# Residual add and RMSNorm on one core: every transfer in 64 KiB runs, a residual area of 9 rows, gamma in PSUM

## The chip, the cores and the metric

The kernel runs on one core of a Trainium2 chip. The metric is the device time of one launch in microseconds (us), the median of several runs. All runs named here are fast, at a granted clock of 1.0, so that they can be compared directly.

## The reference

```python
# x, residual: (32, 2048, 2048) float32; gamma: (2048,) float32; eps = 1e-6
z = x + residual
rms = np.sqrt(np.mean(z ** 2, axis=-1, keepdims=True) + eps)
return (z / rms * gamma).astype(np.float32)
```

There are 65,536 rows of 2048 elements. Two tensors of 537 MB are read and one is written, 1610.6 MB in all.

## The kernel before

A tile is 8 rows on each of 128 partitions, 64 KiB per partition; there are 64 tiles. SBUF holds two z slots (x arrives in one, is worked on in place, and is stored from it) and one residual slot, 192 KiB of each partition; there is no third z slot and no second residual slot. All large transfers go out from one queue, SP's, in program order.

```python
z_slots = [slots.tile([P, R, D], fp32, name=f"z{k}") for k in range(2)]   # R = 8, D = 2048
r_slot = slots.tile([P, R, D], fp32, name="r_slot")
gamma_tile = slots.tile([P, D], fp32, name="gamma_tile")
# ... cut
def load_r(i):
    nc.sync.dma_start(out=r_slot, in_=r_t[i])              # 64 KiB run per partition
def load_x(i):                                             # two halves of 32 KiB
    z = z_slots[i % 2]
    for h in range(2):
        s = slice(h * H, (h + 1) * H)                      # H = 4
        nc.sync.dma_start(out=z[:, s, :], in_=x_t[i][:, s, :])
def compute(i):
    z = z_slots[i % 2]
    for h in range(2):
        s = slice(h * H, (h + 1) * H)
        nc.vector.tensor_add(out=z[:, s, :], in0=z[:, s, :], in1=r_slot[:, s, :])
        # ... cut: 4 squares with a sum on ScalarE, then a square root
    for h in range(2):
        # ... cut: reciprocal, then 4 in-place multiplications by rstd and gamma on VectorE
# ... cut: the first two tiles
for i in range(1, n_tiles):
    store(i - 1)
    compute(i)
    if i + 1 < n_tiles:
        load_r(i + 1)      # waits until the adds of tile i have read r_slot
        load_x(i + 1)      # waits until store(i - 1) has left the z slot
store(n_tiles - 1)
```

In the steady state the DMA engines work through a round of three things per tile: x of tile i, the store of tile i-1, the residual of tile i+1. When x of tile i has landed, the store of tile i-1 is the only work left in the queue until the residual load is issued, and that waits for the adds.

Of the kernel before, what the change touches and what calls it, by code (L numbers as in the profile page):

```python
# [1 line left out]

# [4 lines left out]


@with_exitstack
def kernel(  # L10
    ctx: ExitStack,
    tc: tile.TileContext,
    x: bass.AP,
    residual: bass.AP,
    gamma: bass.AP,
    eps: float,
    out: bass.AP,
):




    nc = tc.nc
    P = nc.NUM_PARTITIONS
    fp32 = mybir.dt.float32
    Act = mybir.ActivationFunctionType
    mult = mybir.AluOpType.mult

    x_f = x.flatten_outer_dims()
    r_f = residual.flatten_outer_dims()  # L30
    o_f = out.flatten_outer_dims()

    n_rows, D = x_f.shape
    R = 8
    H = R // 2
    assert n_rows % (P * R) == 0
    n_tiles = n_rows // (P * R)
    assert n_tiles >= 3

    x_t = x_f.rearrange("(n p r) m -> n p r m", p=P, r=R)  # L40
    r_t = r_f.rearrange("(n p r) m -> n p r m", p=P, r=R)
    o_t = o_f.rearrange("(n p r) m -> n p r m", p=P, r=R)

    inv_d = 1.0 / float(D)

    slots = ctx.enter_context(tc.tile_pool(name="slots", bufs=1))
    stats = ctx.enter_context(tc.tile_pool(name="stats", bufs=3))
    psum = ctx.enter_context(tc.tile_pool(name="psum", bufs=1, space=bass.MemoryType.PSUM))

    z_slots = [slots.tile([P, R, D], fp32, name=f"z{k}") for k in range(2)]  # L50
    r_slot = slots.tile([P, R, D], fp32, name="r_slot")
    gamma_tile = slots.tile([P, D], fp32, name="gamma_tile")
    eps_tile = slots.tile([P, 1], fp32, name="eps_tile")
    sq_junk = psum.tile([P, D], fp32, name="sq_junk")
    nc.vector.memset(eps_tile, float(eps))  # L55

    def load_r(i):
        nc.sync.dma_start(out=r_slot, in_=r_t[i])  # L58

    def load_x(i):  # L60
        z = z_slots[i % 2]
        for h in range(2):
            s = slice(h * H, (h + 1) * H)
            nc.sync.dma_start(out=z[:, s, :], in_=x_t[i][:, s, :])  # L64

    def store(i):
        z = z_slots[i % 2]
        if i < n_tiles - 1:
            nc.sync.dma_start(out=o_t[i], in_=z)
            return  # L70
        for h in range(2):
            s = slice(h * H, (h + 1) * H)
            nc.sync.dma_start(out=o_t[i][:, s, :], in_=z[:, s, :])

    def compute(i):
        z = z_slots[i % 2]
        rstds = []
        for h in range(2):
            s = slice(h * H, (h + 1) * H)
            nc.vector.tensor_add(out=z[:, s, :], in0=z[:, s, :], in1=r_slot[:, s, :])  # L80
            ssq = stats.tile([P, H], fp32, name=f"ssq{h}")
            for g in range(H):
                nc.scalar.activation(  # L83
                    out=sq_junk,
                    in_=z[:, h * H + g, :],
                    func=Act.Square,
                    accum_out=ssq[:, g : g + 1],
                )
            rms = stats.tile([P, H], fp32, name=f"rms{h}")
            nc.scalar.activation(out=rms, in_=ssq, func=Act.Sqrt, bias=eps_tile, scale=inv_d)  # L90
            rstds.append((rms, stats.tile([P, H], fp32, name=f"rstd{h}")))
        for h in range(2):
            rms, rstd = rstds[h]
            nc.vector.reciprocal(out=rstd, in_=rms)  # L94
            for g in range(H):
                row = z[:, h * H + g, :]
                nc.vector.scalar_tensor_tensor(  # L97
                    out=row,
                    in0=row,
                    scalar=rstd[:, g : g + 1],  # L100
                    in1=gamma_tile,
                    op0=mult,
                    op1=mult,
                )


    def load_gamma():
        nc.vector.memset(gamma_tile, 0.0)  # L108
        for q in range(4):
            nc.scalar.dma_start(  # L110
                out=gamma_tile[32 * q : 32 * q + 1, :], in_=gamma.partition_broadcast(1)
            )
        nc.vector.stream_shuffle(gamma_tile, gamma_tile, [0] * 32)  # L113

    load_r(0)
    load_x(0)
    load_gamma()
    load_x(1)
    compute(0)
    load_r(1)  # L120
    for i in range(1, n_tiles):
        store(i - 1)
        compute(i)
        if i + 1 < n_tiles:
            load_r(i + 1)
            load_x(i + 1)
    store(n_tiles - 1)


# [1 line left out]
_INS = ['x', 'residual', 'gamma', 'eps']  # L131
_OUTS = [((32, 2048, 2048), 'float32')]

_NUMBERS = {'eps': 9.999999974752427e-07}


# [26 lines left out]
```

## Time and profile before

| what | value |
|---|---|
| time, median of 3 runs | 3733.61 us (3733.6 to 3735.15) |
| VectorE / ScalarE busy | 62% / 29% |
| SP's DMA queue | 99.9% of the 16 engines' span |
| one steady round (25.17 MB) | 58.06 us |

Three lines of the page: the DMA's busy tenths in 40 slices of the span, the GB/s in the same slices, and the SP queue (packets, MB, share of the 16 engines' span).

```profile
DMA  9999999999999999999999999999999999999999
GB/s 425 414 437 430 435 433 431 435 435 432 433 431 435 436 430 437 429 436 433 431 436 430 437 432 431 437 430 439 430 432 434 432 437 431 430 435 436 431 435 389
...
q1 hardware_dynamic: 37008, 1610.63, 99.9%
```

The DMA is busy in every slice and moves about 433 GB/s in the middle. The kernel is bound by moving bytes.

The timeline of one steady round. The columns are start, duration, engine (SPq is SP issuing a transfer), source line, operation, tiles, and in brackets the idle time before and what ended it.

```profile
1831.38 8.69 DVE L80 TENSOR_TENSOR z<-z,r_slot 128x8192 f32<-128x8192 f32 x1 [1.01 <-DMA z<-in_x_dram]
...
1840.11 0.33 SPq L58 DMA_DIRECT2D r_slot<-in_residual_dram  x1
...
1850.70 0.80 SPq L64 DMA_DIRECT2D z<-in_x_dram  x2
...
1858.63 0.34 SPq L69 DMA_DIRECT2D out_dram<-z  x1
1879.84 8.69 DVE L80 TENSOR_TENSOR z<-z,r_slot 128x8192 f32<-128x8192 f32 x1 [21.24 <-DMA z<-in_x_dram]
...
1889.45 8.69 DVE L80 TENSOR_TENSOR z<-z,r_slot 128x8192 f32<-128x8192 f32 x1 [0.91 <-DMA z<-in_x_dram]
```

The second half of x has landed at 1831.38 and its add takes 8.69 us. The residual load (L58) is issued right behind it, 8.7 us after the add's start. The x loads (L64) follow when the old store is done, the next store (L69) at 1858.63, and at 1889.45 the round begins again, 58.07 us later.

### The profile page before, as it was taken

The numbers are of one execution on the slowest core, as the hardware profiler recorded it, in microseconds if no ns is written. First come the engines' busy times: TensorE is split into PE (matmuls) and PEld (weight loads), VectorE is DVE, ScalarE is ACT, GpSimd is POOL, SyncE is SP. The second block draws the span as 40 slices with busy tenths as digits, with TensorE's granted clock in tenths as the row PEclk, the third lists the DMA queues.
The fourth block names the chain that finished last, engine by engine and source line by source line (L and its number), as shares of the span: only waits on it lengthen the run. The fifth ranks groups of instructions, "written<-read, shape, count | busy, mean of one in ns | idle before, by whom it ended". The sixth has DMA issues, their size and how long they took to land.

```text
span 3732.7 us, 2427 instructions
## 1 busy us (share of the span) xinstructions
DVE 2298.0 (62%) x772; ACT 1066.4 (29%) x1154; POOL 0.2 (0%) x4
## 2 busy tenths in 40 slices
DVE  5665655656557565575655756657566575665756
ACT  2331322313223132231322313323233232331322
POOL 0000000000000000000000000000000000000000
DMA  9999999999999999999999999999999999999999
GB/s 425 414 437 430 435 433 431 435 435 432 433 431 435 436 430 437 429 436 433 431 436 430 437 432 431 437 430 439 430 432 434 432 437 431 430 435 436 431 435 389
DMA packets 37035, 1610.82 MB, mean 432 GB/s; under 512 B 4116, under 2 KB 4116, under 8 KB 4116
## 3 DMA queue, kind: packets, MB, share of 16 engines
q1 hardware_dynamic: 37008, 1610.63, 99.9%
q14 instruction: 19, 0.16, 0.0%
q10 hardware_dynamic: 8, 0.03, 0.0%
HBM read 1073.77 MB, written 536.87 MB: 431 GB/s over the span
## 4 chain that ended last, share of the span: by engine, by line
DMA 66%; another core or an unknown queue 16%; DVE 16%; SPq 1%; ACT 0%; issue 0%; DVEq 0%
DMA z<-in_x_dram 64%; DVE z L80 15%; DMA out_dram<-z 1%; DVE z L97 1%; DMA r_slot<-in_residual_dram 1%; SPq L64 1%; SPq L58 0%; ACT sq_junk L83 0%; DVE rstd L94 0%; DVEq L158 0%; ACT L90 0%; ACT rms L90 0%; DVEq L80 0%
## 5 line engine op out<-in xcount | busy, mean ns | idle before, releaser
L80 DVE TENSOR_TENSOR z<-z,r_slot 128x8192 f32<-128x8192 f32 x128 | 1112.5, 8692 | 1395.0 <-DMA z<-in_x_dram 1382.5
L83 ACT ACTIVATE sq_junk<-z 128x2048 f32<-128x2048 f32 x512 | 963.5, 1882 | 2635.0 <-DVE z L80 2622.9
L97 DVE SCALAR_TENSOR_TENSOR z<-z,rstd,gamma_tile 128x2048 f32<-128x2048 f32 x512 | 1169.9, 2348 | 4.5
L83 ACT ACTIVATION_READ_ACCUMULATOR sq_junk<-z 128x1 f32 x512 | 95.8, 187 | 0.0
L90 ACT ACTIVATE rms<-ssq,eps_tile 128x4 f32<-128x4 f32 x128 | 38.1, 298 | 4.1
L94 DVE RECIPROCAL rstd<-rms 128x4 f32<-128x4 f32 x128 | 21.9, 171 | 0.1
L113 DVE LOAD_MASK_SELECT gamma_tile<-gamma_tile x1 | 0.0, 14 | 21.2 <-DMA gamma_tile<-in_gamma_dram 21.2
L83 ACT ACT_TABLE_LOAD x1 | 1.3, 1283 | 4.4 <-issue 4.4
L113 DVE STREAM_SHUFFLE gamma_tile<-gamma_tile 128x2048 f32<-128x2048 f32 x1 | 2.4, 2419 | 0.0
L108 DVE MEMSET gamma_tile<- 128x2048 f32 x1 | 1.8, 1765 | 0.4 <-issue 0.4
L90 ACT ACT_TABLE_LOAD x1 | 1.3, 1283 | 0.0
L55 DVE MEMSET eps_tile<- 128x1 f32 x1 | 0.1, 59 | 0.8 <-PEq L144 0.8
L144 POOL MEMSET const-bfloat16-1.0<- 128x1 bf16 x1 | 0.1, 103 | 0.0
L144 POOL MEMSET const-uint8-127<- 128x1 uint8 x1 | 0.1, 103 | 0.0
L144 POOL MEMSET const-float32-1.0<- 128x1 f32 x1 | 0.1, 100 | 0.0
L144 POOL MEMSET const-float32-0.0<- 128x1 f32 x1 | 0.1, 99 | 0.2 <-issue 0.2
## 6 DMA issues: line engine op xcount, KB each, us to landing
z<-in_x_dram SPq DMA_DIRECT2D x128, 4096.0 KB, 38.3
out_dram<-z SPq DMA_DIRECT2D x2, 4096.0 KB
r_slot<-in_residual_dram SPq DMA_DIRECT2D x64, 29.9
out_dram<-z SPq DMA_DIRECT2D x63, 50.1
gamma_tile<-in_gamma_dram ACTq DMA_DIRECT2D x4, 8.0 KB
```

The lines of the kernel that those rows point to most:

```text
L55: nc.vector.memset(eps_tile, float(eps))
L64: nc.sync.dma_start(out=z[:, s, :], in_=x_t[i][:, s, :])
L80: nc.vector.tensor_add(out=z[:, s, :], in0=z[:, s, :], in1=r_slot[:, s, :])
L83: nc.scalar.activation(out=sq_junk, in_=z[:, h * H + g, :], func=Act.Square, accum_out=ssq[:, g : g + 1],)
L90: nc.scalar.activation(out=rms, in_=ssq, func=Act.Sqrt, bias=eps_tile, scale=inv_d)
L94: nc.vector.reciprocal(out=rstd, in_=rms)
L97: nc.vector.scalar_tensor_tensor(out=row, in0=row, scalar=rstd[:, g : g + 1], in1=gamma_tile, op0=mult, op1=mult,)
L108: nc.vector.memset(gamma_tile, 0.0)
L113: nc.vector.stream_shuffle(gamma_tile, gamma_tile, [0] * 32)
L144: nc = _bacc.Bacc("TRN2", target_bir_lowering=False, num_devices=1)
```

## The change

The intent is to make every large transfer one 64 KiB run per partition, so x now comes in one piece. The add can then no longer begin at the first half, and the residual load would come very late. So the residual area gets a ninth row: tiles use its rows 0 to 7 and 1 to 8 in turn, and the one row that the next load does not overwrite is added last. The load has to wait for 7 rows instead of 8. The extra row takes the SBUF of gamma, which moves to PSUM. The first and the last tile are cut into pieces of 2 rows.

```diff
-    r_slot = slots.tile([P, R, D], fp32, name="r_slot")
-    gamma_tile = slots.tile([P, D], fp32, name="gamma_tile")
+    r_area = slots.tile([P, R + 1, D], fp32, name="r_area")
+    gamma_tile = psum.tile([P, D], fp32, name="gamma_tile")
     def load_r(i):
-        nc.sync.dma_start(out=r_slot, in_=r_t[i])
+        a = i % 2
+        nc.sync.dma_start(out=r_area[:, a : a + R, :], in_=r_t[i])
-    def load_x(i):
+    def load_x(i, piece=R):
         z = z_slots[i % 2]
-        for h in range(2):
-            s = slice(h * H, (h + 1) * H)
+        for a in range(0, R, piece):
+            s = slice(a, a + piece)
             nc.sync.dma_start(out=z[:, s, :], in_=x_t[i][:, s, :])
     def compute(i):
+        if i % 2 == 0:
+            order = list(range(1, R)) + [0]
+            add(i, 1, R)
+            add(i, 0, 1)
+        else:
+            order = list(range(R))
+            add(i, 0, R - 1)
+            add(i, R - 1, R)
+        groups = (order[:4], order[4:])
+        rms = [square(i, g) for g in groups]
+        for g, m in zip(groups, rms):
+            scale(i, g, m)
# ... cut: add, square and scale as functions, the old body of compute,
#     gamma staged in the area's last row, the first and last tile by pieces of 2 rows
```

More of the change, by code (lines that the diff above doesn't have):

```diff
@@ L34 @@
     R = 8
-    H = R // 2
     assert n_rows % (P * R) == 0
@@ L46 @@
     slots = ctx.enter_context(tc.tile_pool(name="slots", bufs=1))
-    stats = ctx.enter_context(tc.tile_pool(name="stats", bufs=3))
+    stats = ctx.enter_context(tc.tile_pool(name="stats", bufs=4))
     psum = ctx.enter_context(tc.tile_pool(name="psum", bufs=1, space=bass.MemoryType.PSUM))
     z_slots = [slots.tile([P, R, D], fp32, name=f"z{k}") for k in range(2)]
-    r_slot = slots.tile([P, R, D], fp32, name="r_slot")
-    gamma_tile = slots.tile([P, D], fp32, name="gamma_tile")
+    r_area = slots.tile([P, R + 1, D], fp32, name="r_area")
@@ L64, in load_x, with store @@
             nc.sync.dma_start(out=z[:, s, :], in_=x_t[i][:, s, :])
-    def store(i):
+    def store(i, piece=R):
         z = z_slots[i % 2]
-        if i < n_tiles - 1:
-            nc.sync.dma_start(out=o_t[i], in_=z)
-            return
-        for h in range(2):
-            s = slice(h * H, (h + 1) * H)
-            nc.sync.dma_start(out=o_t[i][:, s, :], in_=z[:, s, :])
-    def compute(i):
-        z = z_slots[i % 2]
-        rstds = []
-        for h in range(2):
-            s = slice(h * H, (h + 1) * H)
-            nc.vector.tensor_add(out=z[:, s, :], in0=z[:, s, :], in1=r_slot[:, s, :])
-            ssq = stats.tile([P, H], fp32, name=f"ssq{h}")
-            for g in range(H):
-                nc.scalar.activation(
-                    out=sq_junk,
-                    in_=z[:, h * H + g, :],
-                    func=Act.Square,
-                    accum_out=ssq[:, g : g + 1],
-                )
-            rms = stats.tile([P, H], fp32, name=f"rms{h}")
-            nc.scalar.activation(out=rms, in_=ssq, func=Act.Sqrt, bias=eps_tile, scale=inv_d)
-            rstds.append((rms, stats.tile([P, H], fp32, name=f"rstd{h}")))
-        for h in range(2):
-            rms, rstd = rstds[h]
-            nc.vector.reciprocal(out=rstd, in_=rms)
-            for g in range(H):
-                row = z[:, h * H + g, :]
-                nc.vector.scalar_tensor_tensor(
-                    out=row,
-                    in0=row,
-                    scalar=rstd[:, g : g + 1],
-                    in1=gamma_tile,
-                    op0=mult,
-                    op1=mult,
-                )
@@ new lines, in store, with add, square @@
+        for a in range(0, R, piece):
+            s = slice(a, a + piece)
+            nc.sync.dma_start(out=o_t[i][:, s, :], in_=z[:, s, :])
+    def add(i, a, b):
+        z = z_slots[i % 2]
+        o = i % 2
+        nc.vector.tensor_add(
+            out=z[:, a:b, :], in0=z[:, a:b, :], in1=r_area[:, a + o : b + o, :]
+        )
+    def square(i, rows):
+        z = z_slots[i % 2]
+        ssq = stats.tile([P, 4], fp32, name="ssq")
+        for k, g in enumerate(rows):
+            nc.scalar.activation(
+                out=sq_junk, in_=z[:, g, :], func=Act.Square, accum_out=ssq[:, k : k + 1]
+            )
+        n = len(rows)
+        rms = stats.tile([P, 4], fp32, name="rms")
+        nc.scalar.activation(
+            out=rms[:, :n], in_=ssq[:, :n], func=Act.Sqrt, bias=eps_tile, scale=inv_d
+        )
+        return rms
@@ new lines, in scale @@
+    def scale(i, rows, rms):
+        z = z_slots[i % 2]
+        n = len(rows)
+        rstd = stats.tile([P, 4], fp32, name="rstd")
+        nc.vector.reciprocal(out=rstd[:, :n], in_=rms[:, :n])
+        for k, g in enumerate(rows):
+            nc.vector.scalar_tensor_tensor(
+                out=z[:, g, :],
+                in0=z[:, g, :],
+                scalar=rstd[:, k : k + 1],
+                in1=gamma_tile,
+                op0=mult,
+                op1=mult,
+            )
+    def compute(i):
+        if i % 2 == 0:
[10 more added lines that the diff above has]
+            scale(i, g, m)
@@ L107, in load_gamma, with compute_by_pieces @@
+    def compute_by_pieces(i):
+        groups = [list(range(a, a + 2)) for a in range(0, R, 2)]
+        before = None
+        for g in groups:
+            add(i, g[0], g[-1] + 1)
+            m = square(i, g)
+            if before is not None:
+                scale(i, *before)
+            before = (g, m)
+        scale(i, *before)
     def load_gamma():
-        nc.vector.memset(gamma_tile, 0.0)
+        stage = r_area[:, R, :]
+        nc.vector.memset(stage, 0.0)
         for q in range(4):
@@ L110, in load_gamma @@
             nc.scalar.dma_start(
-                out=gamma_tile[32 * q : 32 * q + 1, :], in_=gamma.partition_broadcast(1)
+                out=r_area[32 * q : 32 * q + 1, R, :], in_=gamma.partition_broadcast(1)
             )
-        nc.vector.stream_shuffle(gamma_tile, gamma_tile, [0] * 32)
+        nc.vector.stream_shuffle(gamma_tile, stage, [0] * 32)
     load_r(0)
-    load_x(0)
+    load_x(0, 2)
     load_gamma()
     load_x(1)
-    compute(0)
+    compute_by_pieces(0)
     load_r(1)
+    last = n_tiles - 1
@@ L121 @@
     for i in range(1, n_tiles):
         store(i - 1)
-        compute(i)
-        if i + 1 < n_tiles:
+        if i < last:
+            compute(i)
             load_r(i + 1)
-            load_x(i + 1)
-    store(n_tiles - 1)
+            load_x(i + 1, 2 if i + 1 == last else R)
+    compute_by_pieces(last)
+    store(last, 2)
 _INS = ['x', 'residual', 'gamma', 'eps']
```

## The prediction

> **What bounds the kernel now.** The DMA engines. The page's slices show DMA at 9 in all 40; its queue table gives the SP queue 99.9% of the 16 engines' span. The chain that ended last is 66% DMA. VectorE is busy 62%, ScalarE 29%. From tile 3 on, the timeline repeats every 58.06 us (59.0 in a few tiles): 25.17 MB per tile, 433 GB/s. The Trainium skill (page "DMA: Bandwidth & Descriptors", section "Where 436 GB/s comes from") puts the ceiling at 435 GB/s; the trace agrees. The same bytes must still move, so little can be won: 1610.6 MB at 435 GB/s is 3701 us (estimate).
>
> **What the change removes.**
> 1. Run length. The packet records show 64 KiB packets at 2418 ns and 32 KiB packets at 1215 ns (medians). A group of 8 x packets and its semaphore write takes 9.70 us on an engine, twice that 19.41; a group of 8 packets of 64 KiB takes 19.32. Only x changes. Saved: about 0.09 us per tile, 62 tiles, 5.5 us, all on the critical path.
> 2. The gap near 100 us. The engines idle 0.7 to 1.7 us there, since the load of r(2) is issued only at 100.42 us, when both adds of tile 1 are done. With 7 rows (about 15.2 us at the measured 8.69 us for 4) in place of 8 (17.3 us) it comes 2 us earlier: about 1 us saved.
> 3. The end. Most engines run dry 7 to 8 us before the last stores, but the two slowest only 1.0 and 2.4 us. With stores of 2 rows the first ones are ready early and the queue never dries: 1 us, set by the slowest engine.
>
> **What it adds.** Shorter runs in the first and last tile: 0.3 us. The scaling reads gamma from PSUM (2.35 us each now): I expect 2.3 to 2.4.
>
> **What it moves.** x arrives as one transfer, so the add can't start at the first half: the residual load is issued about 15.8 us after x has landed, against 8.7 now, and its first packet follows about 1 to 1.5 us later. Meanwhile the store of the tile before keeps the queue fed for 19.3 us. The slack shrinks from about 9 to some 2 us. The slowest engine should not idle; engines that run ahead by more than 2 us will, harmlessly, but pulled together they may stall each other more, as they do in the first 500 us (extra 0.2 to 1 us on first packets of x). Allowance: 0 to 4 us. The tile's store is issued about 42 us after x lands (27 now), still before the DMA needs it at 58.
>
> **Predicted:** 3733.6 - 5.5 - 1 - 1 + 0.3 + about 1 = 3727 us; 8 in 10 between 3721 and 3733. Faster by over 2%: 1%; within 2%: 97%; slower by over 2%: 2%.
>
> **What would show it.** Step 1: packets down from 37,035 to about 29,000 and a period near 57.97 us between the large adds. Step 2: no idle near 100 us. Step 3: all engines busy through the last 20 us, DMA 9 in the last slice, last store landing about 40 us after the last x piece. Slack: residual loads issued 15 to 16 us after the large add starts; DMA share still 1.00 in the middle.
>
> **What would make it wrong.** The residual load waiting for both adds, or for ScalarE (1 us dry in each tile is 1.7%); stalls from engines held in step; or 64 KiB loads of x being slower than those of the residual.

## The result, and the profile after

| | before | after |
|---|---|---|
| median | 3733.8 us | 3796.97 us |
| range, 6 runs each | 3733.6 to 3735.15 | 3793.44 to 3801.55 |
| ratio | | 1.0169 (95% interval 1.0156 to 1.0182) |

Ratios here and below are the mean time of one kernel's fast runs over that of the other's of the same rounds, so they are not quite the ratio of the medians. The change made the kernel 1.7% slower: 63 us more, and 70 us above the prediction and well outside its range. The interval is clear of 1.

The same three lines of the page after the change:

```profile
DMA  9999999999999999999999999999999999999999
GB/s 419 427 425 430 430 430 428 418 429 424 421 422 423 428 420 426 426 418 428 429 427 426 417 423 426 422 425 424 425 423 424 429 428 425 424 418 424 420 424 403
...
q1 hardware_dynamic: 28944, 1610.63, 99.7%
```

Fewer packets move the same bytes, as intended, and the DMA is still busy in every slice. Only the rate has fallen, to about 424 GB/s. The busy share hides the loss, because a packet that is held up counts as busy. The windows view of the long middle stretch says it more plainly (stretch, length, the busy time and count of VectorE, ScalarE and GpSimd, granted clock, DMA share, GB/s), before and then after:

```profile
1000.00:3000.00 2000.00, 1232.92 (x410) 571.77 (x619) 0.00 (x0) 1.00 1.00 434
```

```profile
1000.00:3000.00 2000.00, 1206.64 (x403) 545.59 (x597) 0.00 (x0) 1.00 1.00 424
```

The DMA share is 1.00 in both, at 434 and 424 GB/s. One steady round after the change:

```profile
1799.65 17.29 DVE L78 TENSOR_TENSOR z<-z,r_area 128x14336 f32<-128x14336 f32 x2 [16.68 <-DMA z<-in_x_dram]
1814.76 0.33 SPq L61 DMA_DIRECT2D r_area<-in_residual_dram  x1
...
1818.96 0.33 SPq L67 DMA_DIRECT2D z<-in_x_dram  x1
...
1841.85 0.34 SPq L73 DMA_DIRECT2D out_dram<-z  x1
1858.55 17.29 DVE L78 TENSOR_TENSOR z<-z,r_area 128x14336 f32<-128x14336 f32 x2 [16.73 <-DMA z<-in_x_dram]
```

The residual load (L61) is now issued 15.1 us after the add's start instead of 8.7, the store 42.2 us instead of 27.2. The large add starts 58.90 us after the last one in this round; the mean over the steady rounds is 59.30 (in the profiled execution, which at 3801.55 us was the slowest of the six).

The packet records (start, duration and size of every packet) and the semaphore writes at the end of each engine's share (a semaphore is the counter that tells the waiting engine that data have landed) say where in the round it goes. From these I took the mean time that the 16 engines need for each transfer. After the change x takes 20.07 us, the store 19.33, the residual 19.91. A clean transfer of this size takes 19.32 to 19.35. So x loses 0.7 us and the residual 0.6 us per round, on all engines and mostly as longer packets: at the start of the residual load, and in the last two or three packets of the x load that comes after it.

The records also show that the 16 engines are not in step. "Spread" below is the time between the first and the last engine's end of the same transfer. "Lead" is the time from the issue of the residual load until the first engine has finished the store in front of it.

| | before | after |
|---|---|---|
| spread, early and late in the run | 1.6 and 7.8 us | 1.4 to 3.3 us, without a trend |
| lead of the residual load over the first engine | 4.6 us (mean) | 1.3 us |
| the same over the slowest engine | 10.1 us | 3.8 us |

The slowest engine always has its next work in time, as the prediction said. The round slows down nevertheless. Hardly any engine even runs dry: the first packet follows 0.96 us after the issue, and in the mean only 0.6 of the 16 engines per round have a lead below that.

### The profile page after: what moved, and what is told of

Read it like the earlier page. It is cut to its first block, busy times and chain, and to the rows that moved or that the text cites. A ratio compares the mean times of both kernels' runs of the same rounds, so it can differ in the third digit from the quotient of the medians.

```text
span 3799.8 us, 2509 instructions
## 1 busy us (share of the span) xinstructions
DVE 2296.1 (60%) x780; ACT 1060.1 (28%) x1158; POOL 0.2 (0%) x4
## 4 chain that ended last, share of the span: by engine, by line
DMA 64%; DVE 29%; ACT 7%; issue 0%; DVEq 0%; SPq 0%
DMA z<-in_x_dram 33%; DMA out_dram<-z 30%; DVE z L102 15%; DVE z L78 13%; ACT sq_junk L86 7%; DMA r_area<-in_residual_dram 1%; ACT rms L91 0%; DVE rstd L100 0%; DVEq L191 0%; ACT L91 0%; DVEq L78 0%; SPq L61 0%; SPq L67 0%
## 5 line engine op out<-in xcount | busy, mean ns | idle before, releaser
L78 DVE TENSOR_TENSOR z<-z,r_area 128x14336 f32<-128x14336 f32 (+2 forms) x132 | 1107.5, 8429 | 1066.6 <-DMA z<-in_x_dram 1049.2
L102 DVE SCALAR_TENSOR_TENSOR z<-z,rstd,gamma_tile 128x2048 f32<-128x2048 f32 x512 | 1167.9, 2343 | 4.5
L100 DVE RECIPROCAL rstd<-rms 128x4 f32<-128x4 f32 (+1 forms) x132 | 22.7, 173 | 391.3 <-ACT rms L91 391.3
L91 ACT ACTIVATE rms<-ssq,eps_tile 128x4 f32<-128x4 f32 (+1 forms) x132 | 39.2, 297 | 4.3
```

Source lines behind the costliest of these rows:

```text
L78: nc.vector.tensor_add(out=z[:, a:b, :], in0=z[:, a:b, :], in1=r_area[:, a + o : b + o, :])
L91: nc.scalar.activation(out=rms[:, :n], in_=ssq[:, :n], func=Act.Sqrt, bias=eps_tile, scale=inv_d)
L100: nc.vector.reciprocal(out=rstd[:, :n], in_=rms[:, :n])
L102: nc.vector.scalar_tensor_tensor(out=z[:, g, :], in0=z[:, g, :], scalar=rstd[:, k : k + 1], in1=gamma_tile, op0=mult, op1=mult,)
```

## The experiments

Theory A: the residual load comes too late. Its rival, theory B: the 64 KiB runs of x are what stalls where the queue turns from loads to stores. Eleven kernels were run, named e1 to e12 (there is no e6). The first four tell the two theories apart. The diffs are shortened: repeated branches and lines of the first tiles are left out.

**e1: x in halves again, the late residual load kept.**

```diff
-            load_x(i + 1, 2 if i + 1 == last else R)
+            load_x(i + 1, 2 if i + 1 == last else R // 2)
```

> The changed kernel with x loaded again as two transfers of 4 rows (32 KiB per partition), and nothing else put back: the add of 7 rows still waits for both, so the residual load is still issued about 15.5 us after x has landed. Theory A (the late residual load: engines that run ahead go dry, are pulled back into step, and all 16 then stall together where the queue turns from loads to stores and back): stays slow, 3780 to 3805 us, spread between the engines 1.5 to 3 us. Theory B (the 64 KiB runs of x are themselves what stalls at the turn): back to 3730 to 3745 us.

Measured: 3803.91 us, ratio 1.0185 (1.0170 to 1.0200). The runs of x were put back and nothing was won. Theory B falls. The load still goes out 15.1 us after the add's start, as this round of e1 shows:

```profile
1866.52 17.29 DVE L78 TENSOR_TENSOR z<-z,r_area 128x14336 f32<-128x14336 f32 x2 [17.73 <-DMA z<-in_x_dram]
1881.64 0.33 SPq L61 DMA_DIRECT2D r_area<-in_residual_dram  x1
```

**e2: x whole, the residual early.**

```diff
     def load_r(i):
-        a = i % 2
-        nc.sync.dma_start(out=r_area[:, a : a + R, :], in_=r_t[i])
+        for h in (0, R // 2):
+            s = slice(h, h + R // 2)
+            nc.sync.dma_start(out=r_area[:, s, :], in_=r_t[i][:, s, :])
     def compute(i):
-        add(i, 1, R); add(i, 0, 1)                  # or 0..7 and 7..8
+        add(i, 0, R // 2); add(i, R // 2, R)
# ... cut: in add, the residual is read from a fixed place
```

> The changed kernel with x still as one transfer of 64 KiB per partition, but the residual at a fixed place, added in two adds of 4 rows and loaded in two transfers of 4 rows, each issued when its add is done: the first about 9 us after x has landed, as early as in the kernel before. Theory A: back to 3722 to 3738 us, the spread between engines grows to 5 us and more. Theory B: stays at 3770 to 3800 us.

Measured: 3729.66 us (3729.32 to 3730.19), ratio 0.9987 (0.9970 to 1.0004). The large runs of x stay and the loss is gone. From the timeline of e2:

```profile
1826.56 17.29 DVE L79 TENSOR_TENSOR z<-z,r_area 128x8192 f32<-128x8192 f32 x2 [22.35 <-DMA z<-in_x_dram]
1835.28 8.93 SPq L62 DMA_DIRECT2D r_area<-in_residual_dram  x2
...
1884.57 17.30 DVE L79 TENSOR_TENSOR z<-z,r_area 128x8192 f32<-128x8192 f32 x2 [22.22 <-DMA z<-in_x_dram]
```

The first half of the residual is issued 8.7 us after the add's start, as early as before the change, and the round is back at 58.0 us. The spread grew to more than 6 us.

**e3: the kernel before, with one add of 8 rows.**

```diff
-            nc.vector.tensor_add(out=z[:, s, :], in0=z[:, s, :], in1=r_slot[:, s, :])
+            if h == 0:
+                nc.vector.tensor_add(out=z, in0=z, in1=r_slot)
```

> The kernel before with only this changed: one add of 8 rows when both halves of x are there, so the residual load is issued about 17.5 us after x has landed instead of 8.7. All runs as in the kernel before (x 32 KiB, the rest 64 KiB). Theory A: as slow as the changed kernel or slower, 3795 to 3900 us. Theory B: 3730 to 3745 us.

Measured: 4011.26 us, ratio 1.0731 (1.0707 to 1.0754). Nothing of the change is in this kernel except the lateness, and it loses 277 us, more than expected. The middle stretch of e3 in the windows view:

```profile
1000.00:3000.00 2000.00, 1146.89 (x353) 528.11 (x576) 0.00 (x0) 1.00 0.96 403
```

Here the engines really are idle at times (share 0.96). The load is issued 1.6 us after the first engine has run dry, yet 1.7 us before the slowest engine is done. Its transfer takes 22.6 us in the mean of all engines. In this, 15 of the 16 wait for their first packet, 2.2 us in the mean; but the slowest one, which has its work in time, takes 22.4 us too instead of 19.3.

**e4: x in halves, each added as it lands, all else as changed.**

```diff
# on top of e1
-            add(i, 1, R)
+            add(i, 1, R // 2)
+            add(i, R // 2, R)
             add(i, 0, 1)
# and in the other branch
-            add(i, 0, R - 1)
+            add(i, 0, R // 2)
+            add(i, R // 2, R - 1)
```

> The changed kernel with x in two halves and the adds split so that each half is added as it lands; gamma in PSUM, the area of 9 rows, and the first and last tile by pieces of 2 rows all stay. The residual load is issued 6.5 to 8.7 us after x has landed. Both theories: 3725 to 3737 us. If it stays above 3745 us, one of the parts left in (gamma in PSUM, the pieces, the area) costs time, and both theories fall.

Measured: 3731.35 us (3731.17 to 3731.5), ratio 0.9991 (0.9976 to 1.0006). The ninth row, gamma in PSUM and the pieces at both ends cost nothing. e1 and e4 differ in when the add begins, and so when the residual goes out: 73 us lie between them. Two rounds of e4, with the load 6.6 and 8.7 us after the start of the last large add:

```profile
1828.29 8.76 DVE L78 TENSOR_TENSOR z<-z,r_area 128x6144 f32<-128x6144 f32 x2 [0.90 <-DMA z<-in_x_dram]
1834.88 0.33 SPq L61 DMA_DIRECT2D r_area<-in_residual_dram  x1
...
1886.45 8.69 DVE L78 TENSOR_TENSOR z<-z,r_area 128x8192 f32<-128x8192 f32 x1 [0.85 <-DMA z<-in_x_dram]
1895.17 0.33 SPq L61 DMA_DIRECT2D r_area<-in_residual_dram  x1
```

The next four ask how the lateness works.

**e5: x as 2 and 6 rows, an intermediate lateness.** The residual lies at a fixed place and the adds follow the pieces.

```diff
-        for a in range(0, R, piece):
-            s = slice(a, a + piece)
+        cuts = [0, 2, R] if piece == R else list(range(0, R + 1, piece))
+        for a, b in zip(cuts, cuts[1:]):
+            s = slice(a, b)
             nc.sync.dma_start(out=z[:, s, :], in_=x_t[i][:, s, :])
# compute: add(i, 0, 2); add(i, 2, R)
```

> The changed kernel with x as two transfers of 2 and 6 rows, added in the same parts as they land, and the residual at a fixed place: the residual load goes out 13.0 us after x has landed, between the 8.7 of the kernel before and the 15.2 of the changed one. Theory A, in the form that it has now: a residual load costs time once it comes later than the moment when the first engine has done the store before it. That is at 19.3 us less its latency (0.96 us in the traces) less the 0.5 us from landing to the add less the spread of the engines: for 13.0 us, only at a spread over 4.9 us. So 3728 to 3740 us, and the spread grows to about 5 us and stays there. If instead the loss grew evenly with the lateness, it would be near 3765 us.

Measured: 3740.34 us, ratio 1.0017 (1.0002 to 1.0032): just over what theory A had, and far from an even growth with lateness. The spread stayed at 3.3 to 4.4 us instead of 5, so the allowance that I had made for the load's latency was too small. The mean lead over the first engine is 2.3 us. Most rounds are clean (median 58.08 us) and some are not (mean 58.30).

**e7: GpSimd adds two of the seven rows.** All runs stay at 64 KiB.

```diff
-            add(i, 1, R)
+            add(i, R - 2, R, nc.gpsimd)
+            add(i, 1, R - 2)
             add(i, 0, 1)
```

> The changed kernel with all runs left at 64 KiB; only 2 of the 7 rows of the large add are given to GpSimd, beside VectorE's 5 (about 10.9 us). If GpSimd's part takes less than that, the residual load goes out 10.9 us after x has landed. Theory A: 3720 to 3730 us, the fastest of all. If the runs of 64 KiB throughout cost anything by themselves: over 3740 us. If GpSimd takes over 15 us for its rows, it stays near 3800 us and tells nothing of the runs.

Measured: 3970.28 us, ratio 1.0634. This is a miss of the design. The groups of e7 by shape (line, engine, operation, tiles, shapes, count, then busy us and mean ns of one):

```profile
L78 POOL TENSOR_TENSOR z<-z,r_area 128x4096 f32<-128x4096 f32 x62 | 1203.8, 19415 | 2680.7 <-DMA z<-in_x_dram 2597.6 <-DMA r_area<-in_residual_dram 83.0
...
L78 DVE TENSOR_TENSOR z<-z,r_area 128x2048 f32<-128x2048 f32 x62 | 676.2, 10906 | 0.0
L78 DVE TENSOR_TENSOR z<-z,r_area 128x10240 f32<-128x10240 f32 x62 | 671.2, 10825 | 1350.6 <-DMA z<-in_x_dram 1333.4 <-DMA r_area<-in_residual_dram 17.2
```

VectorE adds 5 rows in 10.8 us, undisturbed. GpSimd, started at the same time, is done only after 19.4 us, 8.6 us after VectorE, and the single row that VectorE adds next takes 10.9 us, where it takes 2.3 alone. So the two worked one after the other. The Trainium skill says this: the page "SBUF — State Buffer", section "Terms", describes a shared port pair that VectorE and GpSimd hold exclusively for a whole instruction, "the loser fully blocks". The trace agrees. The residual load went out later than in the changed kernel, so e7 says nothing about the runs.

**e8: a late store.** e4 with VectorE work that changes nothing.

```diff
         for n, (g, m) in enumerate(zip(groups, rms)):
             scale(i, g, m)
+            if n == 0:
+                z, a = z_slots[i % 2], min(g)
+                for _ in range(2):
+                    nc.vector.tensor_max(z[:, a : a + 4, :], z[:, a : a + 4, :], z[:, a : a + 4, :])
```

> Run e4 (x in halves, early residual load, 3731 us) with 17 us of extra VectorE work that changes nothing, after half of the scaling: the store of each tile is issued about 45 us after x has landed, some 13 us before the DMA needs it (42 and 16 in the changed kernel). Rival theory C: it is not the residual load but the store that comes late, and the loss at the end of x, just before the store's turn, is its mark: 3760 to 3800 us. Theory A: stays at 3728 to 3736 us.

Measured: 3731.56 us, ratio 0.9993. The later store of the changed kernel is not the cause, and 17 us more of VectorE's work in each tile shows no cost, although part of the loss appears just before the store's turn.

**e9: late in one tile of four.**

```diff
# on top of e4, even tiles
+            if i % 4 == 0:
+                add(i, 1, R)
+            else:
                 add(i, 1, R // 2)
                 add(i, R // 2, R)
             add(i, 0, 1)
```

> Run e4 with the undivided add of 7 rows put back in every fourth tile alone, so that one residual load in four is late. All four late cost 72 us (run e1 against e4). Theory A, if a late load costs time only in its own round: a quarter, so 3745 to 3752 us. If the engines, once brought into step, go on stalling for several tiles: 3755 to 3800 us. If they keep enough spread between the late loads for these to do nothing: under 3737 us.

Measured: 3752.48 us, ratio 1.0053 (1.0036 to 1.0070). That is 21 us above e4 for 15 late loads, 1.4 us each. The timeline of e9 shows one cycle; each round ends at an add that waited for the second half of x (in even rounds the large add, in the others the second L78 line):

```profile
1428.68 15.09 DVE L78 TENSOR_TENSOR z<-z,r_area 128x14336 f32<-128x14336 f32 x1 [7.31 <-DMA z<-in_x_dram]
...
1443.80 0.33 SPq L61 DMA_DIRECT2D r_area<-in_residual_dram  x1
...
1488.10 8.76 DVE L78 TENSOR_TENSOR z<-z,r_area 128x6144 f32<-128x6144 f32 x2 [1.75 <-DMA z<-in_x_dram]
...
1494.68 0.33 SPq L61 DMA_DIRECT2D r_area<-in_residual_dram  x1
...
1546.19 8.69 DVE L78 TENSOR_TENSOR z<-z,r_area 128x8192 f32<-128x8192 f32 x1 [0.92 <-DMA z<-in_x_dram]
...
1604.30 8.76 DVE L78 TENSOR_TENSOR z<-z,r_area 128x6144 f32<-128x6144 f32 x2 [0.98 <-DMA z<-in_x_dram]
...
1662.50 15.09 DVE L78 TENSOR_TENSOR z<-z,r_area 128x14336 f32<-128x14336 f32 x1 [7.48 <-DMA z<-in_x_dram]
```

From 1428.68, where the late load follows, to 1488.10 it takes 59.42 us. The next three rounds take 58.09, 58.11 and 58.20. Over the whole run, rounds with a late load take 59.61 us, the rounds right after them 58.12, all others 58.11. The loss is made in the late load's own round and does not carry on.

The last three measure what was left in dispute.

**e10: all runs at 64 KiB and an early load.** Only the first 4 rows get their residual. Its output is wrong, which doesn't matter for the time.

```diff
# on top of e2
-        for h in (0, R // 2): ...
+        nc.sync.dma_start(out=r_area[:, 0:R, :], in_=r_t[i])
-        add(i, 0, R // 2)
-        add(i, R // 2, R)
+        add(i, 0, R // 2)  # wrong on purpose: the other rows get no residual
```

> All three streams with 64 KiB runs and an early residual load, which no correct version so far has both of: the residual at a fixed place, and only the first 4 rows of a tile get it, so that the load goes out about 9 us after x has landed. The result is wrong on purpose in the steady tiles; transfers, bytes and order are the changed kernel's. It measures what the prediction put at 5.5 us (0.09 us per tile): 0.09 x 62 below runs e2 and e4 (3729.7 and 3731.4, each with one stream of 32 KiB runs), so 3722 to 3727 us. If runs of 64 KiB throughout stall by themselves: 3740 us or more.

Measured: 3725.29 us (3725.18 to 3726.28), ratio 0.9977 (0.9963 to 0.9990). It moves the changed kernel's transfers in its order and is 72 us faster. It also leaves out half of VectorE's adds; e2, which has them all, shows the same 19.36 us for x. The middle of e10 in the windows view:

```profile
1000.00:3000.00 2000.00, 933.64 (x375) 566.50 (x617) 0.00 (x0) 1.00 1.00 434
```

The middle runs at 434 GB/s, with x at 19.35, the store at 19.33 and the residual at 19.32 us. The mean steady round is 58.00 us, against 58.09 before the change and 59.30 after it.

**e11: the store at the last moment.**

```diff
# on top of e2, in the scaling loop
             scale(i, g, m)
+            if n == 0:
+                for _ in range(2):
+                    nc.vector.tensor_max(z[:, 0:4, :], z[:, 0:4, :], z[:, 0:4, :])
```

> Run e2 (3729.7 us) with 17.4 us of extra VectorE work that changes nothing, so that the store of a tile goes out about 53 us after x has landed, 0 to 2 us before the first engine has done its load of the next x. The residual load stays early. If the loss belongs to any transfer that reaches the queue less than about 2 us before the first engine needs it: 1 us or more per tile, 3775 to 3830 us. If it belongs to the residual load alone (a load behind a store): 3728 to 3738 us.

Measured: 3748.58 us, ratio 1.0037 (1.0023 to 1.0051). This lies between the two expectations. The store's mean lead over the first engine is 1.5 us, and the round takes 58.40 us against 58.11 in e2. So a late store behind a load costs too, but 0.3 us, where a residual load behind a store with a lead of 1.3 us costs 1.2 to 1.3. Why the two differ is open.

**e12: gamma back in SBUF, area of 8 rows.** e2 without the change of gamma's place.

```diff
# on top of e2
-    r_area = slots.tile([P, R + 1, D], fp32, name="r_area")
-    gamma_tile = psum.tile([P, D], fp32, name="gamma_tile")
+    r_area = slots.tile([P, R, D], fp32, name="r_area")
+    gamma_tile = slots.tile([P, D], fp32, name="gamma_tile")
```

> Run e2 with gamma back in SBUF and the residual area at 8 rows, so that what is left of the change is x in one transfer, the first and last tile by pieces, and the residual in two loads. Gamma's place should not matter, since VectorE is off the bound: 3728 to 3732 us, the scaling 2.34 to 2.35 us in both. It also times this version against the kernel before in five rounds.

Measured: 3730.22 us in five rounds, ratio 0.9989 (0.9975 to 1.0002). Gamma's place does not matter. e2 and e12 are the fastest correct versions: all their runs (3729.3 to 3730.3 us) lie below all runs of the kernel before (3733.5 to 3735.4), by 4 to 5 us, though the interval of the ratio just includes 1.

**All rounds together.** The leads differ from round to round, so the rounds of before, after, e1, e3, e4, e5 and e9 can be sorted by the residual load's lead over the first engine, leaving out the ends of each run. A round is timed from the slowest engine's end of one store to that of the next.

| lead over the first engine | rounds | mean round |
|---|---|---|
| 2.25 us and more | 190 | 58.1 to 58.2 us |
| 2.0 to 2.25 | 13 | 58.4 |
| 1.5 to 2.0 | 48 | 58.9 |
| 1.25 to 1.5 | 28 | 59.3 |
| 0 to 1.25 | 63 | 59.5 to 59.7 |
| under 0 (e3 alone: 15 of 16 engines dry) | 56 | 62.4 |

This is a comparison of rounds, not an experiment of its own, but it agrees with e3, e5 and e9, where the lead was set on purpose. It also holds within one kernel: in e5 the lead over the slowest engine is 5.8 to 6.2 us in all rounds, and the third of them with the smallest lead over the first engine (1.8 us in the mean) takes 58.65 us, the others 58.13. So the moment of the issue alone does not set the loss. Here the residual load has to be issued about 2.2 us before the first engine ends its store. That is nearly the 2.4 us of one 64 KiB packet, but no run varied the packets of the store, so that the two belong together is not shown.

## Why the prediction was wrong

*What bounds the kernel: right.* It is the DMA. The Trainium skill's ceiling of 435 GB/s (page "DMA: Bandwidth & Descriptors", section "Where 436 GB/s comes from") agrees with the 434 GB/s of e10. The same section says that for transfers between HBM (the chip's main memory) and SBUF, as these are, an HBM limit of about 358 GB/s binds instead; on this one core it did not, and the measurement decides.

*Step 1, the run length: right.* Predicted 0.09 us per tile. e10's round is 0.09 us shorter than that of before (58.00 against 58.09). The 8.9 us between their medians also hold the gap of step 2.

*Step 2, the gap near 100 us: right.* The load of tile 2's residual was issued 1.7 us earlier. By the packet records the engines stand idle here for 1.05 us in the mean before the change, 0.24 us after it and not at all in e10, whose load is earlier still. So 0.8 of the predicted 1 us was won. (The windows view cannot tell this: it counts a packet whole where it starts, and in a stretch of 5 us, two packets long, it gives the DMA a share of 0.88 before and 0.83 after.) The two issues, before and then after:

```profile
100.42 0.33 SPq L58 DMA_DIRECT2D r_slot<-in_residual_dram  x1
```

```profile
98.74 0.33 SPq L61 DMA_DIRECT2D r_area<-in_residual_dram  x1
```

*Step 3, the end: no gain.* From the slowest engine's last x piece to the end of the span it is 40.3 us before, 40.4 after and 40.5 in e10. The queue no longer dries, but the 1 us did not show.

*What it adds: right for gamma.* Scaling takes 2343 ns with gamma in PSUM and 2348 with gamma in SBUF. The 0.3 us for shorter runs at both ends was not measured on its own.

*What it moves: this step failed.* The times were right: the load was put at 15.8 us after landing, and 15.1 us after the add's start (about 15.5 after landing) was measured. Its first packet follows after 0.96 us in an empty queue (100.42 to 101.38 before the change, and 0.96 on average in e3). The Trainium skill gives about 0.6 us to the first byte for this kind of issue (same page, section "Latency and other measured facts"); the trace agrees if one counts from the end of the issuing instruction, which takes 0.33 us and leaves 0.63. The slack of "some 2 us" was even too small: the slowest engine has a lead of 3.8 us, or 2.8 after the 0.96. What failed is the sentence "The slowest engine should not idle; engines that run ahead by more than 2 us will, harmlessly", and the "Allowance: 0 to 4 us" that rested on it. The slowest engine indeed did not idle. But the engines are not independent. When a late load leaves the first engine less than about 2.2 us, all of them lose time in that round, by longer packets more than by idling. The prediction named stalls between the engines as a risk, but the term was put at 0 to 4 us for the whole run. Measured, it is 1.30 us per round (59.30 against e10's 58.00), and 72 us between the medians of the two kernels.

The check that I had named for it, "DMA share still 1.00 in the middle", was met and proved nothing. GB/s was the number to look at.

My first form of theory A said that the stalls come because the engines are pulled into step. That form does not hold: the rounds of e9 without a late load run at a spread of 2.0 to 3.4 us, like those of the changed kernel, and lose nothing. What stays is the lead.

What stays open is why the packets stall. The skill says that descriptors of one queue start in order but are pipelined, with separate read and write sides ("DMA: Bandwidth & Descriptors", section "Two DMAs through the same engine are not ordered"). A need to have the next packet at hand about one packet early would fit with that, but no run here shows the inside of an engine. Nor do the runs explain why the second part of the loss comes only some 36 us later, at the end of x, or why a late store costs less than a late load.

## What to carry to other kernels

When a kernel is bound by DMA, count the time from the issue of each transfer to the moment when the first of the 16 engines needs it, not the slowest, and keep a reserve (here about 2.2 us; one packet takes 2.4); merging transfers to save 0.09 us per tile cost 1.3 us here because it delayed the wait that issues the next one. Read GB/s, since a DMA that is busy all the time can still be slowed. If a large piece must stay whole, split the transfer behind the wait instead: x whole and the residual in two loads gave 3729.7 us.

## What the Trainium skill lacked or had wrong

- "DMA: Bandwidth & Descriptors" says nothing of how early a transfer must be queued behind another to keep the rate. Here it is about 2.2 us ahead of the first engine's end with 64 KiB packets; below that a round of 58.1 us grows to 59.6, and to 62.4 once 15 of the 16 engines are dry (e3).
- The same page says that the 16 engines finish independently. Their ends do lie up to 8 us apart here, but their rates are not independent, of which the page has nothing: in e3 the slowest engine had a lead of 1.7 us, more than the 0.96 us from issue to first packet, and still took 22.4 us for the transfer instead of 19.3.
- The same page's section "Where 436 GB/s comes from" says without a condition that about 358 GB/s of HBM bind transfers between HBM and SBUF. Here one core moved 434 GB/s between them for 2000 us (e10). No run used a second core.
- The same page gives about 0.6 us from issue to first byte and not from which moment it counts. Measured to the first packet on an idle engine, it is 0.96 us from the start of the issuing instruction and 0.63 from its end.
- The same page speaks of a cost per packet for small transfers only. Two packets of 32 KiB take 2 x 1215 ns and one of 64 KiB takes 2418 (medians): 12 ns per extra run on an engine, and 0.09 us per tile with the extra semaphore write.
